# One feature-first token tile instead of two, in the value and output projections of a hybrid decoder layer

## The chip, the core and the metric

The kernel runs on one core of one Trainium2 chip. The time is the device time of one execution in microseconds. Five engines work side by side: TensorE (PE, with its weight loads PEld), VectorE (DVE), ScalarE (ACT), GpSimd (POOL) and SyncE (SP), which issues the transfers.

## The reference

One layer of a decoder is computed for 512 prompt tokens and 8 sample tokens, model width 1024. An input projection gives, per token, queries, keys, values and a gate for two mixers. Mixer A is gated linear attention (4 heads, keys of 64, values of 128, `va` with 512 columns), mixer B is dilated sliding-window attention (8 heads of 64, `vb` with 512 columns), for the samples against a cache of past keys and values. Each mixer's output is multiplied by the SiLU of its gate, the two are put side by side, and an output projection of 1024 x 1024, a residual and a LayerNorm follow:

```
h = x @ w_in;  qa, ka, va, za, ga, qb, kb, vb, gb = split(h)
o_a = rms_norm(gla(qa, ka, va, log_a(za))) ;  o_b = dilated_attention(qb, kb, vb)
y = concat(o_a * silu(ga), o_b * silu(gb)) @ w_out
x_new = layer_norm(ALPHA * x + y) ;  also out: new GLA states, kb, vb
```

## The kernel before

All operands lie in fast memory once loaded; x stands transposed, 1024 features in eight groups of 128 partitions, and 520 columns of tokens: prompt tiles 0 and 1 (256), the 8 samples, prompt tiles 2 and 3 (256). The first 264 columns are `TS[0]`, the last 256 `TS[1]`.

Precision comes from splitting: every weight and activation is a sum of a high and a low part, and each product is three matmuls (`three`, L622): high by high, high by low, low by high. So one unit of a projection is 8 x 3 = 24 matmuls that add up in one bank of the accumulator memory.

A unit has one of two forms. *Features first*: 128 weight columns are the stationary operand, the tokens move, and the result stands with features on the partitions. *Tokens first*: 128 tokens are stationary, 256 or 512 weight columns move, and the result stands with tokens on the partitions. Queries, keys and gates are features first throughout. The values are wanted tokens first for the prompt, but features first for the samples. `token` (L640) makes a group of 256 value columns (there are two of mixer B, `vb`, and two of mixer A, `va`): two units features first over `TS[0]`, whose prompt part of 256 columns `turn` (L659) copies out and turns by two transposes on TensorE, and two units tokens first for tiles 2 and 3. `va_into` and `vb_into` (L1085, L1102) copy the results to where the mixers read them; `vb_into` also splits them and stores them.

The output projection has the same two forms. `out_first` (L1512) runs eight units features first over tiles 0 and 1 and the samples (`ps_yf`), the first five of them in two halves: their products with mixer B's outputs ahead of all products with mixer A's. `out_turn` (L1533) copies, turns and adds them to the residual. `out_unit` (L1500) makes tiles 2 and 3 tokens first (`ps_y`, 512 or 256 columns); `out_evac` adds a result to the residual and takes its statistics; `norm` finishes a tile.

The generator `dense` (L695) gives the order of TensorE's large work: first keys and queries, then qb, kb, vb, gb, va, ga, then the output projection. All other work (decay, levels, scores, softmax, samples) stands in generators of its own with a priority from the table `PRIO` (L72). A planner (`Plan.run`, L308) builds the program: it keeps an estimated clock for each engine, charges each operation a cost (for a matmul in L120), and at each step records the operation that can start first, the smaller number in `PRIO` first among equals. `FROM_POOL` and `LATE` (L76, L78) are two of its waiting times. What it records is the fixed order on each engine; L368 is the line that records, and so nearly every row of the profile has that line. Accumulator banks have tags: three of "d" and three of "s" for products and scores, two of "t" for transposes and small results; the transposes of the probabilities (`ps_pt`) are of the latter.

Of the kernel before, what the change touches and what calls it, by code (L numbers as in the profile page):

```python
# [20 lines left out]
P = 128  # L21
# [48 lines left out]


PRIO = dict(  # L72
    wload=3, wsplit=4, decay=48.3, res_s=8, res=8, level=22, keys_out=2, logit=25.7, value=20, fills=9, bias_table=7.3, gla_levels=7.6, gla_diagonal=7.7, gla_state=24, gla_queries=25, strips=14, sample_queries=48, sample_softmax=8.7, sample_values=46, sample_gla=11, mix_sample_a=8.7, mix_sample_b=16, ln_rows=17, keys_store=17.5, gla_out=26, sample_v=9.2, mix_tiles=33.5, scores=31, softmax=34.2, weighted=30, mix_a=18, mix_b=19, norm3=11, norm=9)


FROM_POOL = 1000.0  # L76
TO_PE, FROM_PE, OTHER, AFTER_DMA, WITHIN = 600.0, 250.0, 150.0, 500.0, 120.0
LATE = 600.0  # L78
SWITCH = 230.0
PIECE = 256  # L80

# [114 lines left out]
class Plan:  # L196
# [14 lines left out]
    def add(self, gen, prio):  # L211
        self.seq += 1
        self.tasks.append(Task(gen, prio, self.seq))

    def mark(self, name):
        self.marks[name] += 1
# [156 lines left out]
def trunk(ctx: ExitStack, tc: tile.TileContext, xT, xp, xs, state, ck, cv, w_in, wab, gnorm,  # L373
# [17 lines left out]
    def bank(tag, name):  # L391
        return Need(tag, name, [P, 512])
# [20 lines left out]
    def copy(o, x):  # L413
        return V.tensor_copy(o, x), S.copy(o, x)
# [36 lines left out]
    def make(key, need, n=1):  # L451

        B[key] = yield need
        if n > 1:
            plan.share(B[key], n)
        mark(key)
# [165 lines left out]
    def three(ps, k, pairs):  # L622
        for i, (l, r) in enumerate(pairs):
            yield T.matmul(ps, l, r, start=k == 0 and i == 0, stop=k == KT - 1 and i == 2)
# [12 lines left out]
            add(evac(ps, u), 2)  # L637
        g.done(0)

    def token(g, evac_f, evac):  # L640

        for f in range(2):
            fs = slice(f * P, f * P + P)
            ps = yield bank("d", f"ps_{g.name}f{f}")
            for k in range(KT):
                yield g.at(k)
                h, l = xh[k][:, TS[0]], xl[k][:, TS[0]]
                yield from three(ps[:, :TW[0]], k, ((g.hi[k][:, fs], h), (g.hi[k][:, fs], l), (g.lo[k][:, fs], h)))
            add(evac_f(ps, f), 2)
        for t in (2, 3):  # L650
            ps = yield bank("d", f"ps_{g.name}{t}")
            ts = slice(NB + t * P, NB + t * P + P)
            for k in range(KT):
                yield from three(ps[:, :GW], k, ((xh[k][:, ts], g.hi[k]), (xh[k][:, ts], g.lo[k]), (xl[k][:, ts], g.hi[k])))
            add(evac(ps[:, :GW], t), 2)
        g.done(0)
        g.done(1)

    def turn(ps):  # L659

        f = yield Need("t1", "feat", [P, GW])
        yield copy(f, ps[:, :GW])
        free(ps)
        o = yield bank("t", "ps_turn")
        for t in range(2):
            yield T.transpose(o[:, t * P:t * P + P], f[:, t * P:t * P + P], ident)
        return o, f

    def sample_rows(x, rows):

# [24 lines left out]
    def dense():  # L695
# [44 lines left out]
        for t in range(TT):  # L740
            add(residual(t), PRIO["res"])
        add(residual_sample(), PRIO["res_s"])
        units = [(g, f) for g in range(4) for f in range(2)]
        yield from out_first(*units[:5])
        for x in units[5:]:
            yield from out_first(x)
        for t, c, w in ((2, 0, 512), (2, 512, 512), (3, 0, 512), (3, 512, GW), (3, 768, GW)):
            yield from out_unit(t, c, w)
# [316 lines left out]
    def keys_store():  # L1065

        yield At("kw", 8)
        yield At("y0_done", 1)
        for i in range(2):
            kw = B[f"kw{i}"].rearrange("p m (b j) -> p m b j", j=32)  # L1070
            for m in range(2):
                for a in range(4):
                    c = (2 * i + m) * P + a * 32
                    yield D.dma_start(kw_p[:, c:c + 32].rearrange("(b i) j -> i b j", i=32), kw[a * 32:a * 32 + 32, m])
            free(B[f"kw{i}"])
# [7 lines left out]
        mark(n + "_out")  # L1083

    def va_into(i):  # L1085
        def evac_f(ps, f):
            c = slice(i * GW + f * P, i * GW + f * P + P)
            yield copy(vat[:, 2 * i + f, :], ps[:, GW:TW[0]])
            mark("vat")
            ps, f_t = yield from turn(ps)  # L1090
            free(f_t)
            yield copy(B["va0"][:, :, c], ps[:, :GW].rearrange("p (t c) -> p t c", t=2))
            mark("va_done")
            free(ps)

        def evac(ps, t):
            yield copy(B["va1"][:, t - 2, i * GW:i * GW + GW], ps)
            free(ps)
            mark("va_done")
        return evac_f, evac  # L1100

    def vb_into(i):  # L1102
        def parts_of(o, x):
            yield S.copy(o[..., 0, :], x)
            yield V.tensor_tensor(o[..., 1, :], x, o[..., 0, :].bitcast(F32), op=ALU.subtract)

        def evac_f(ps, f):
            c = slice(i * GW + f * P, i * GW + f * P + P)
            yield copy(vnt[:, 2 * i + f, :], ps[:, GW:TW[0]])
            mark("vnt")  # L1110
            ps, raw = yield from turn(ps)
            yield from parts_of(B[f"vhl{i}0"][:, :, 2 * f:2 * f + 2], ps[:, :GW].rearrange("p (t h d) -> p t h d", t=2, d=64))
            mark(f"vb{i}0")
            yield copy(raw, ps[:, :GW])
            free(ps)
            yield D.dma_start(vw_p[:GW, c].rearrange("(t p) c -> p t c", p=P), raw.rearrange("p (t c) -> p t c", t=2))
            free(raw)

        def evac(ps, t):
            yield from parts_of(B[f"vhl{i}1"][:, t - 2], ps.rearrange("p (h d) -> p h d", d=64))  # L1120
            mark(f"vb{i}1")
            raw = yield Need("t1", "vb_raw", [P, GW])
            yield copy(raw, ps)
            free(ps)
            yield D.dma_start(vw_p[t * P:t * P + P, i * GW:i * GW + GW], raw)
            free(raw)
        return evac_f, evac


    def strips():  # L1130
# [347 lines left out]


    def ln_rows():  # L1480
        yield At("y0_done", 1)
        for n, src in (("gamma", ln_g), ("beta", ln_b)):
            B[n] = yield Need("g", n, [P, DM])
            yield D.dma_start(B[n], src.to_broadcast([P, DM]))
            mark("ln")
        yield S.mul(B["gamma"], B["gamma"], -0.5)
        mark("ln")
# [9 lines left out]
        yield D.dma_start(y, xp[t * P:t * P + P, :])  # L1497
        mark(f"y{t}")

    def out_unit(t, c, w):  # L1500
        u, tl, cs = t // 2, slice((t % 2) * P, (t % 2) * P + P), slice(c % 512, c % 512 + w)
        g = wo[c // 512]
        ps = yield bank("d", f"ps_y{t}{c // GW}")
        for k in range(KT):
            yield g.at(k)
            yield At(f"mix_b{u}{k}") if k < 4 else At(f"mix_a{u}", t % 2 + 1)
            mh, ml = (B[f"m{x}{'ba'[k // 4]}{u}"][:, k % 4, tl] for x in "hl")
            hi, lo = g.hi[k][:, cs], g.lo[k][:, cs]
            yield from three(ps[:, :w], k, ((mh, hi), (mh, lo), (ml, hi)))
        add(out_evac(t, c // GW, ps[:, :w]), 2)  # L1510

    def out_first(*units):  # L1512


        ps = []
        for g, f in units:
            ps.append((yield bank(("d", "s"), f"ps_yf{g}{f}")))
            yield from out_half(g, f, ps[-1], range(4))
        for (g, f), p in zip(units, ps):
            yield from out_half(g, f, p, range(4, KT))  # L1520
            add(out_turn(g, f, p), 2)

    def out_half(g, f, ps, ks):
        w, c = wo[g // 2], g % 2 * GW + f * P
        for k in ks:
            yield w.at(k)
            yield At(f"mix_b0{k}") if k < 4 else At("mix_a0", 2)
            yield At(f"mix_s{'ba'[k // 4]}")
            mh, ml = (B[f"m{x}{'ba'[k // 4]}0"][:, k % 4, :] for x in "hl")
            hi, lo = w.hi[k][:, c:c + P], w.lo[k][:, c:c + P]  # L1530
            yield from three(ps[:, :TW[0]], k, ((hi, mh), (lo, mh), (hi, ml)))

    def out_turn(g, f, ps):  # L1533
        feat = yield Need("t1", "feat_y", [P, GW])
        yield copy(feat, ps[:, :GW])
        yield copy(yts[:, 2 * g + f, :], ps[:, GW:TW[0]])
        mark("yts")
        free(ps)
        if f == 0:
            yield from make(f"yt{g}", bank("t", f"ps_yt{g}"))  # L1540
        else:
            yield At(f"yt{g}")
        for t in range(2):
            yield T.transpose(B[f"yt{g}"][:, t * GW + f * P:t * GW + f * P + P], feat[:, t * P:t * P + P], ident)
        free(feat)
        mark(f"yt_in{g}")
        if plan.marks[f"yt_in{g}"] == 2:
            plan.share(B[f"yt{g}"], 2)
            for t in range(2):
                add(out_evac(t, g, B[f"yt{g}"][:, t * GW:t * GW + GW]), 2)  # L1550

    def out_evac(t, g, ps):
        yield At(f"y{t}")
# [218 lines left out]
```

## Time and profile before

| | |
|---|---|
| time, median of 3 runs | 288.28 us (288.16 to 288.7) |
| the profiled execution, its own time | 287.84 us |
| its span, first to last instruction | 286.1 us |
| TensorE busy | 274.8 us, 96%, 2638 matmuls |
| VectorE busy | 223.5 us, 78% |
| ScalarE busy | 172.1 us, 60% |
| GpSimd busy | 59.6 us, 21% |
| mean granted TensorE clock | 0.997 of full speed |

A row of the profile that groups or lists instructions has the engine, the operation, what it writes `<-` what it reads, and the size: `128*128` is the stationary operand in rows and columns, `128x264` the partitions and columns that a matmul writes. A matmul's recorded duration contains the way through its pipeline, and several are under way at once; how fast they follow is the distance from start to start. The chain that ended last lists pieces of the critical chain as start, length, engine, tile and number of instructions.

### The profile page before, as it was taken

How to read it: one execution, taken by the hardware profiler on the slowest of the kernel's cores; microseconds unless marked ns; L12 is line 12 of the kernel's file. 1: busy time of each engine (PE TensorE's matmuls, PEld its weight loads, DVE VectorE, ACT ScalarE, POOL GpSimd, SP SyncE). 2: the span in 40 equal slices, each digit the busy share in tenths (PEclk: the TensorE clock that was granted, in tenths of full speed). 3: DMA queues.
4: the chain of work that ended last, by engine and by line, in shares of the span. 5: the costliest groups of instructions: out<-in, count | busy, mean ns of one | idle time of the engine just before them, and what ended most of it. 6: DMA issues, size and time to landing. Idle time of an engine off the chain costs nothing.

```text
span 286.1 us, 6902 instructions
## 1 busy us (share of the span) xinstructions
PE 274.8 (96%) x2638; PEld 259.1 (91%) x2638; DVE 223.5 (78%) x546; ACT 172.1 (60%) x481; POOL 59.6 (21%) x74
## 2 busy tenths in 40 slices
PE   8999999999999999999999999899999999999991
PEld 5999999999989899998999999799899999997890
DVE  4923887899999989989889897765698895439845
ACT  5726565456877887696888685435689774212002
POOL 4000000002945907200047635540000000000000
PEclk9999999999999999999999999999999999999998
DMA  6963643337738687527996858768193796751112
GB/s 205 341 167 93 203 111 105 91 110 221 244 88 297 194 256 240 159 83 214 264 235 200 261 157 231 198 169 229 52 255 115 208 313 236 124 170 73 78 76 92
DMA packets 58371, 51.20 MB, mean 179 GB/s; under 512 B 12750, under 2 KB 49752, under 8 KB 58338
## 3 DMA queue, kind: packets, MB, share of 16 engines
q1 hardware_dynamic: 57778, 50.36, 59.7%
q8 instruction: 21, 0.34, 0.5%
q10 hardware_dynamic: 560, 0.39, 0.4%
q14 instruction: 12, 0.10, 0.1%
HBM read 45.19 MB, written 6.05 MB: 179 GB/s over the span
## 4 chain that ended last, share of the span: by engine, by line
PE 67%; DVE 17%; ACT 9%; DMA 3%; issue 1%; SPq 1%; DVEq 0%; ACTq 0%
PE ps_qb L368 8%; PE ps_y L368 8%; PE ps_yf L368 7%; PE ps_gb L368 6%; PE ps_first L368 5%; PE ps_vb_f L368 4%; PE ps_vb L368 4%; PE ps_va L368 3%; PE ps_pv L368 3%; PE ps_pt L368 3%; PE ps_kb L368 2%; PE ps_qa L368 2%; ACT sg L368 2%; PE ps_s L368 2%; DMA raw_wo__3550<-in_w_out_dram 2%
## 5 line engine op out<-in xcount | busy, mean ns | idle before, releaser
L368 POOL TENSOR_TENSOR past<-past,qbc 128x256 f32<-128x256 f32 x32 | 29.0, 941 | 78.5 <-DMA past<-in_ck_dram 78.5
L368 POOL TENSOR_TENSOR vv<-vv,pb 128x256 f32<-128x256 f32 x32 | 26.3, 853 | 47.5 <-DVE gb_s L368 30.6
L368 ACT ACTIVATE pr<-pr,ms 128x128 f32<-128x128 f32 (+3 forms) x59 | 30.8, 548 | 4.5 <-DVE ms L368 4.4
L368 PE MATMUL ps_first<-xx,hi_first 128*128 128x264 f32 (+1 forms) x96 | 18.2, 289 | 0.4 <-DVE xx L368 0.3
L368 PEld LDWEIGHTS ps_first<-xx,hi_first 128*128 128x128 f32 x96 | 15.0, 190 | 1.4 <-DVE xx L368 0.5
L368 PE MATMUL ps_pt<-cf,pr 128*128 128x128 f32 x80 | 13.8, 280 | 1.2 <-DVE va L368 0.6
L368 DVE CUSTOM_DVE_ANT_0 pr<-ps_s,strip 128x128 f32<-128x128 f32 (+3 forms) x32 | 14.3, 479 | 0.0
L368 PE MATMUL ps_first<-xx,lo_first 128*128 128x264 f32 (+1 forms) x48 | 13.5, 282 | 0.0
L368 ACT ACTIVATE sg<-sg 128x264 f32<-128x264 f32 (+1 forms) x32 | 13.4, 418 | 0.2
L368 ACT ACTIVATE rstd<-mv,eps 128x1 f32<-128x1 f32 x4 | 1.1, 291 | 18.6 <-DVE mv L368 18.6
L368 PEld LDWEIGHTS ps_pt<-cf,pr 128*128 128x128 f32 x80 | 9.1, 140 | 2.4 <-ACT pr L368 1.2
L368 DVE TENSOR_TENSOR ptl<-ps_pt,pth 128x384 fp32r<-128x384 f32 (+1 forms) x16 | 9.7, 618 | 1.9 <-ACT pth L368 1.8
L368 ACT ACTIVATE d<-d 128x512 f32<-128x512 f32 x13 | 7.7, 636 | 5.1 <-DVE d L368 5.1
L368 DVE TENSOR_REDUCE o_pv<-vv 128x4 f32<-128x1024 f32 x8 | 9.7, 1212 | 0.6 <-POOL vv L368 0.6
L368 DVE TENSOR_REDUCE lt<-past 128x16 f32<-128x1024 f32 x8 | 9.6, 1210 | 0.0
L368 DVE TENSOR_TENSOR d<-b 128x1024 f32<-128x1024 f32 x7 | 9.0, 1290 | 0.0
L368 DVE TENSOR_TENSOR obT<-ps_pv,pvl 64x256 f32<-64x256 f32 x16 | 6.6, 415 | 3.0 <-ACT pvl L368 2.9
L368 PEld LDWEIGHTS ps_first<-xx,lo_first 128*128 128x128 f32 x48 | 9.0, 188 | 0.0
L368 ACT COPY feat_y<-ps_yf 128x256 f32<-128x256 f32 x7 | 2.6, 373 | 10.6 <-PE ps_yf L368 10.6
L368 PE MATMUL ps_s<-kp,qh 64*128 64x128 f32 (+3 forms) x64 | 8.5, 345 | 0.0
L368 ACT CAST pth<-ps_pt 128x384 fp32r<-128x384 f32 (+1 forms) x16 | 8.2, 532 | 0.1
L368 PE MATMUL ps_pv<-pth,vhl 128*128 128x256 f32 (+1 forms) x32 | 7.7, 272 | 0.0
(542 smaller groups left out, 1067.8 us busy)
## 6 DMA issues: line engine op xcount, KB each, us to landing
past<-in_ck_dram SPq DMA_DIRECT2D x8, 512.0 KB
vv<-in_cv_dram SPq DMA_DIRECT2D x8, 512.0 KB, 4.9
pb<-psd_s SPq DMA_DIRECT2D x16, 256.0 KB, 4.2
qbc<-qsd SPq DMA_DIRECT2D x8, 256.0 KB, 5.5
strip<-tabr SPq DMA_DIRECT2D x8, 256.0 KB, 3.1
y<-in_xp_dram SPq DMA_DIRECT2D x4, 512.0 KB
x_raw<-in_xT_dram SPq DMA_DIRECT2D x7, 260.0 KB
out_dram<-y SPq DMA_DIRECT2D x3, 512.0 KB, 2.6
```

What stands on the lines that cost most here:

```text
L368: getattr(eng.eng, op.fn)(*op.args, **op.kw)
```

## The change

The feature-first units of the values and of the output projection cover tile 1 and the samples, 136 columns, where they covered tiles 0 and 1 and the samples, 264. Tile 0 is made tokens first. `turn` now handles 128 prompt columns and one transpose; two feature units of a group share one accumulator bank for their transposes, and one evacuation of 256 columns follows. In the output projection the first five units are tile 0's first 512 columns and feature units 0 to 3, the other five tile 0's second 512 columns and feature units 4 to 7. Two waits on `y0_done` count to 3 in place of 1. All entries of `PRIO` but one and two of the planner's waiting times have other values, and the fixed order of every engine is recorded anew.

```diff
 PRIO = dict(
-    wload=3, wsplit=4, decay=48.3, res_s=8, res=8, level=22, keys_out=2, logit=25.7, value=20, fills=9, bias_table=7.3, gla_levels=7.6, gla_diagonal=7.7, ...
+    wload=12.1, wsplit=5.9, decay=31.1, res_s=18.3, res=28.2, level=22.5, keys_out=2, logit=35.7, value=28.9, fills=59.4, bias_table=37.7, gla_levels=11.8, gla_diagonal=17.1, ...
-FROM_POOL = 1000.0
+FROM_POOL = 300.0
-LATE = 600.0
+LATE = 900.0
...
-    def token(g, evac_f, evac):
+    def token(g, own, evac):
         for f in range(2):
             fs = slice(f * P, f * P + P)
             ps = yield bank("d", f"ps_{g.name}f{f}")
             for k in range(KT):
                 yield g.at(k)
-                h, l = xh[k][:, TS[0]], xl[k][:, TS[0]]
-                yield from three(ps[:, :TW[0]], k, ((g.hi[k][:, fs], h), (g.hi[k][:, fs], l), (g.lo[k][:, fs], h)))
-            add(evac_f(ps, f), 2)
-        for t in (2, 3):
+                h, l = xh[k][:, P:TW[0]], xl[k][:, P:TW[0]]
+                yield from three(ps[:, :P + NB], k, ((g.hi[k][:, fs], h), (g.hi[k][:, fs], l), (g.lo[k][:, fs], h)))
+            add(turn(g.name, ps, f, own[:, f, :], evac), 2)
+        for t in (0, 2, 3):
...
-    def turn(ps):
-        f = yield Need("t1", "feat", [P, GW])
-        yield copy(f, ps[:, :GW])
+    def turn(n, ps, f, own, evac):
+        feat = yield Need("t1", "feat", [P, P])
+        yield copy(feat, ps[:, :P])
+        yield copy(own, ps[:, P:P + NB])
+        mark("vnt" if n[1] == "b" else "vat")
         free(ps)
-        o = yield bank("t", "ps_turn")
-        for t in range(2):
-            yield T.transpose(o[:, t * P:t * P + P], f[:, t * P:t * P + P], ident)
-        return o, f
+        if f == 0:
+            yield from make("turn_" + n, bank("t", "ps_turn"))
+        else:
+            yield At("turn_" + n)
+        o = B["turn_" + n]
+        yield T.transpose(o[:, f * P:f * P + P], feat, ident)
+        free(feat)
+        if f:
+            add(evac(o[:, :GW], 1), 2)
...
-        units = [(g, f) for g in range(4) for f in range(2)]
-        yield from out_first(*units[:5])
-        for x in units[5:]:
+        yield from out_first((0, 0), 0, 1, 2, 3)
+        for x in ((0, 512), 4, 5, 6, 7):
             yield from out_first(x)
...
     def out_first(*units):
         ps = []
-        for g, f in units:
-            ps.append((yield bank(("d", "s"), f"ps_yf{g}{f}")))
-            yield from out_half(g, f, ps[-1], range(4))
-        for (g, f), p in zip(units, ps):
-            yield from out_half(g, f, p, range(4, KT))
-            add(out_turn(g, f, p), 2)
+        for ks in range(4), range(4, KT):
+            for i, x in enumerate(units):
+                if ks[0] == 0:
+                    ps.append((yield bank(("d", "s"), f"ps_yf{i}")))
+                if isinstance(x, tuple):
+                    yield from out_unit(*x, 512, ps[i], ks)
+                else:
+                    yield from out_half(x, ps[i], ks)
...
-            yield from three(ps[:, :TW[0]], k, ((hi, mh), (lo, mh), (hi, ml)))
+            yield from three(ps[:, :P + NB], k, ((hi, mh), (lo, mh), (hi, ml)))
```

The recorded order shows the new sequence. On TensorE, around the turns of the first group of mixer B's values (`ps_vb_f` is the second feature unit, `ps_vb_2` and `ps_vb_0` are token units of tiles 2 and 0, `xx` are the parts of x, `hi_vb` and `lo_vb` those of the weights), before:

```order
L368 MATMUL ps_vb_f_1630<-xx_179,hi_vb__1212 128x264
L368 MATMUL ps_turn<-cf,feat 128x128 x2
L368 MATMUL ps_vb_f_1630<-xx_178,lo_vb__1213 128x264
...
L368 MATMUL ps_vb_f_1630<-xx_263,lo_vb__1433 128x264
L368 MATMUL ps_vb_2_1684<-hi_vb__1212,xx_107 128x256
...
L368 MATMUL ps_turn<-cf,feat 128x128 x2
L368 MATMUL ps_vb_2_1684<-hi_vb__1432,xx_219 128x256
```

And with the change:

```order
L368 MATMUL ps_vb_f_1622<-xx_219,lo_vb__1449 128x136
L368 MATMUL ps_turn<-cf,feat 128x128
L368 MATMUL ps_vb_f_1622<-xx_219,hi_vb__1448 128x136
...
L368 MATMUL ps_vb_f_1622<-xx_263,lo_vb__1449 128x136
L368 MATMUL ps_vb_0_1660<-hi_vb__1318,xx_107 128x256
...
L368 MATMUL ps_turn<-cf,feat 128x128
L368 MATMUL ps_vb_0_1660<-hi_vb__1318,xx_178 128x256
```

Nine matmuls of the second feature unit and nine of tile 0's unit now stand between the two transposes; before, two transposes stood at each place, with the rest of the unit and half of tile 2's between. Over the four groups TensorE has 192 matmuls of 136 columns in place of 192 of 264, 96 more of 256, and 8 transposes fewer.

On TensorE, where the output projection begins (`mhb`, `mlb` are the parts of mixer B's gated outputs, `ps_oat` turns mixer A's), before:

```order
L368 MATMUL ps_yf_3652<-mhb_2263,hi_wo__3318 128x264
L368 MATMUL ps_yf_3652<-mhb_2263,lo_wo__3319 128x264
L368 MATMUL ps_yf_3652<-mlb_2264,hi_wo__3318 128x264
...
L368 MATMUL ps_oat<-cf,oa_3144 128x128 x8
L368 MATMUL ps_yf_3686<-mlb_2264,hi_wo__3336 128x264
...
L368 MATMUL ps_yf_3652<-mha_3608,hi_wo__3502 128x264
```

And with the change:

```order
L368 MATMUL ps_yf_3732<-hi_wo__3441,mhb_2261 128x512
L368 MATMUL ps_yf_3732<-lo_wo__3442,mhb_2261 128x512
L368 MATMUL ps_yf_3732<-hi_wo__3441,mlb_2262 128x512
...
L368 MATMUL ps_oat<-cf,oa_3238 128x128 x8
...
L368 MATMUL ps_yf_3790<-mhb_2261,hi_wo__3441 128x136
...
L368 MATMUL ps_yf_3732<-hi_wo__3628,mha_3700 128x512
```

The first unit is tile 0's first half, tokens first (the outputs are now the stationary operand), and four of 136 columns follow before mixer A's products. Over the projection there are 192 matmuls of 136 columns in place of 192 of 264, 48 more of 512, and 8 transposes fewer.

More of the change, by code (lines that the diff above doesn't have):

```diff
@@ L72 @@
 PRIO = dict(
-    wload=3, wsplit=4, decay=48.3, res_s=8, res=8, level=22, keys_out=2, logit=25.7, value=20, fills=9, bias_table=7.3, gla_levels=7.6, gla_diagonal=7.7, gla_state=24, gla_queries=25, strips=14, sample_queries=48, sample_softmax=8.7, sample_values=46, sample_gla=11, mix_sample_a=8.7, mix_sample_b=16, ln_rows=17, keys_store=17.5, gla_out=26, sample_v=9.2, mix_tiles=33.5, scores=31, softmax=34.2, weighted=30, mix_a=18, mix_b=19, norm3=11, norm=9)
-FROM_POOL = 1000.0
+    wload=12.1, wsplit=5.9, decay=31.1, res_s=18.3, res=28.2, level=22.5, keys_out=2, logit=35.7, value=28.9, fills=59.4, bias_table=37.7, gla_levels=11.8, gla_diagonal=17.1, gla_state=27, gla_queries=21.6, strips=26.7, sample_queries=8.4, sample_softmax=8.4, sample_values=38.6, sample_gla=7.7, mix_sample_a=4.9, mix_sample_b=14.8, ln_rows=8.4, keys_store=17.1, gla_out=17.7, sample_v=26.4, mix_tiles=27.7, scores=39.6, softmax=27.8, weighted=50.7, mix_a=38.6, mix_b=57.6, norm3=8.7, norm=15.3)
+FROM_POOL = 300.0
 TO_PE, FROM_PE, OTHER, AFTER_DMA, WITHIN = 600.0, 250.0, 150.0, 500.0, 120.0
-LATE = 600.0
+LATE = 900.0
 SWITCH = 230.0
@@ L646, in token @@
                 yield g.at(k)
-                h, l = xh[k][:, TS[0]], xl[k][:, TS[0]]
-                yield from three(ps[:, :TW[0]], k, ((g.hi[k][:, fs], h), (g.hi[k][:, fs], l), (g.lo[k][:, fs], h)))
-            add(evac_f(ps, f), 2)
-        for t in (2, 3):
+                h, l = xh[k][:, P:TW[0]], xl[k][:, P:TW[0]]
+                yield from three(ps[:, :P + NB], k, ((g.hi[k][:, fs], h), (g.hi[k][:, fs], l), (g.lo[k][:, fs], h)))
+            add(turn(g.name, ps, f, own[:, f, :], evac), 2)
+        for t in (0, 2, 3):
             ps = yield bank("d", f"ps_{g.name}{t}")
-            ts = slice(NB + t * P, NB + t * P + P)
+            o = NB * (t > 1) + t * P
+            ts = slice(o, o + P)
             for k in range(KT):
@@ L1067, in keys_store @@
         yield At("kw", 8)
-        yield At("y0_done", 1)
+        yield At("y0_done", 3)
         for i in range(2):
@@ L1085, in va_into, with evac @@
     def va_into(i):
[L1086 to L1094, printed above, removed]
         def evac(ps, t):
-            yield copy(B["va1"][:, t - 2, i * GW:i * GW + GW], ps)
+            yield copy(B[f"va{t // 2}"][:, t % 2, i * GW:i * GW + GW], ps)
             free(ps)
             mark("va_done")
-        return evac_f, evac
+        return vat[:, 2 * i:2 * i + 2, :], evac
     def vb_into(i):
-        def parts_of(o, x):
+        def evac(ps, t):
+            o, x = B[f"vhl{i}{t // 2}"][:, t % 2], ps.rearrange("p (h d) -> p h d", d=64)
             yield S.copy(o[..., 0, :], x)
             yield V.tensor_tensor(o[..., 1, :], x, o[..., 0, :].bitcast(F32), op=ALU.subtract)
[L1107 to L1121, printed above, removed]
+            mark(f"vb{i}{t // 2}")
             raw = yield Need("t1", "vb_raw", [P, GW])
@@ L1126, in evac @@
             free(raw)
-        return evac_f, evac
+        return vnt[:, 2 * i:2 * i + 2, :], evac
     def strips():
@@ L1480, in ln_rows @@
     def ln_rows():
-        yield At("y0_done", 1)
+        yield At("y0_done", 3)
         for n, src in (("gamma", ln_g), ("beta", ln_b)):
@@ L1498, in residual, with out_unit @@
         mark(f"y{t}")
-    def out_unit(t, c, w):
+    def out_unit(t, c, w, ps=None, ks=range(KT)):
         u, tl, cs = t // 2, slice((t % 2) * P, (t % 2) * P + P), slice(c % 512, c % 512 + w)
         g = wo[c // 512]
-        ps = yield bank("d", f"ps_y{t}{c // GW}")
-        for k in range(KT):
+        ps = ps or (yield bank("d", f"ps_y{t}{c // GW}"))
+        for k in ks:
             yield g.at(k)
@@ L1509, in out_unit, with out_half @@
             yield from three(ps[:, :w], k, ((mh, hi), (mh, lo), (ml, hi)))
-        add(out_evac(t, c // GW, ps[:, :w]), 2)
+        if KT - 1 in ks:
+            add(out_evac(t, c // GW, ps[:, :w]), 2)
     def out_first(*units):
         ps = []
-        for g, f in units:
-            ps.append((yield bank(("d", "s"), f"ps_yf{g}{f}")))
-            yield from out_half(g, f, ps[-1], range(4))
-        for (g, f), p in zip(units, ps):
-            yield from out_half(g, f, p, range(4, KT))
-            add(out_turn(g, f, p), 2)
-    def out_half(g, f, ps, ks):
-        w, c = wo[g // 2], g % 2 * GW + f * P
+        for ks in range(4), range(4, KT):
[6 more added lines that the diff above has]
+                    yield from out_half(x, ps[i], ks)
+    def out_half(m, ps, ks):
+        w, c = wo[m // 4], m % 4 * P
         for k in ks:
@@ L1528, in out_half, with out_turn @@
             yield At(f"mix_s{'ba'[k // 4]}")
-            mh, ml = (B[f"m{x}{'ba'[k // 4]}0"][:, k % 4, :] for x in "hl")
+            mh, ml = (B[f"m{x}{'ba'[k // 4]}0"][:, k % 4, P:] for x in "hl")
             hi, lo = w.hi[k][:, c:c + P], w.lo[k][:, c:c + P]
-            yield from three(ps[:, :TW[0]], k, ((hi, mh), (lo, mh), (hi, ml)))
[L1533 to L1536, printed above, removed]
+            yield from three(ps[:, :P + NB], k, ((hi, mh), (lo, mh), (hi, ml)))
+        if KT - 1 in ks:
+            add(out_turn(m, ps), 2)
+    def out_turn(m, ps):
+        feat = yield Need("t1", "feat_y", [P, P])
+        yield copy(feat, ps[:, :P])
+        yield copy(yts[:, m, :], ps[:, P:P + NB])
         mark("yts")
         free(ps)
-        if f == 0:
-            yield from make(f"yt{g}", bank("t", f"ps_yt{g}"))
-        else:
-            yield At(f"yt{g}")
-        for t in range(2):
-            yield T.transpose(B[f"yt{g}"][:, t * GW + f * P:t * GW + f * P + P], feat[:, t * P:t * P + P], ident)
+        n = f"yt{m // 2}"
+        if m % 2 == 0:
+            yield from make(n, bank("t", "ps_" + n))
+        else:
+            yield At(n)
+        yield T.transpose(B[n][:, m % 2 * P:m % 2 * P + P], feat, ident)
         free(feat)
[L1546 to L1550, printed above, removed]
+        mark(n + "_in")
+        if plan.marks[n + "_in"] == 2:
+            add(out_evac(1, m // 2, B[n][:, :GW]), 2)
     def out_evac(t, g, ps):
```

## The prediction

> **What bounds the kernel now.** I read the page's busy shares first, then TensorE's waits, then the busy time by stage, then the chain that ended last.
>
> ```profile
> PE 274.8 (96%) x2638; PEld 259.1 (91%) x2638; DVE 223.5 (78%) x546; ACT 172.1 (60%) x481; POOL 59.6 (21%) x74
> PEclk9999999999999999999999999999999999999998
> ```
>
> TensorE (PE) works almost from end to end at its full granted clock, and there are as many weight loads (PEld) as matmuls: each of the 2638 matmuls brings its own stationary operand in, even where two in a row use the same one. The next view is who TensorE waited for.
>
> ```profile
> PE ps_va_f L368 <- DVE lo_va__2973 L368: 1.2, 2, 1.0
> PE warm_ps L368 <- DVE warm L1640: 1.2, 1, 1.2
> PE ps_pt L368 <- DVE va L368: 0.6, 1, 0.6
> PE ps_oa L368 <- DVE oa L368: 0.6, 1, 0.6
> PE ps_pt L368 <- DVE pt L368: 0.5, 1, 0.5
> PE ps_first L368 <- DVE xx L368: 0.3, 1, 0.3
> PE ps_yf L368 <- DVE ga L368: 0.3, 1, 0.3
> ```
>
> That is every wait over 150 ns: 1.2 + 1.2 + 0.6 + 0.6 + 0.5 + 0.3 + 0.3 = 4.7 us in all, 1.8 of it around the GLA values (the first and third rows). So TensorE is the bound in every stage; VectorE is the next one. The stages (values of mixer B 93.5 to 126.5, values of mixer A 162.5 to 195.5, output projection 232.7 to 278.8, then the tail):
>
> ```profile
> core 0: us, PE busy (x) PEld busy (x) DVE busy (x) ACT busy (x) POOL busy (x), PEclk, DMA share, GB/s
> 93.50:126.50 33.00, 32.97 (x281) 31.78 (x282) 29.34 (x84) 26.99 (x84) 13.85 (x16) 1.00 0.64 197
> 126.50:162.50 36.00, 36.00 (x299) 33.84 (x299) 32.13 (x83) 29.07 (x74) 11.43 (x14) 1.00 0.76 214
> 162.50:195.50 33.00, 31.13 (x257) 30.19 (x255) 25.15 (x44) 18.07 (x46) 14.91 (x19) 1.00 0.72 203
> 195.50:232.70 37.20, 36.43 (x343) 34.93 (x341) 30.55 (x107) 29.41 (x106) 0.00 (x0) 1.00 0.64 175
> 232.70:278.80 46.10, 46.03 (x311) 42.04 (x312) 29.11 (x76) 10.71 (x32) 0.00 (x0) 1.00 0.46 145
> 278.80:286.10 7.30, 0.99 (x10) 0.42 (x9) 4.13 (x9) 1.64 (x6) 0.00 (x0) 0.89 0.26 90
> ```
>
> In the stages that the change touches TensorE is idle for 0.03, 1.87 and 0.07 us. Whatever the change adds to TensorE's stream there lengthens the run, up to those waits.
>
> **The price of one matmul.** A matmul's recorded duration contains its pipeline, so I price by distance from start to start, taken from unbroken pieces of the chain that ended last (start, length, matmuls).
>
> ```profile
> 99.78 1.58 PE ps_vb_f L368 x13
> 101.35 1.42 PE ps_vb L368 x12
> 142.35 0.44 PE ps_pt L368 x4
> 240.61 1.46 PE ps_yf L368 x12
> 242.28 1.45 PE ps_yf L368 x12
> 261.81 16.97 PE ps_y L368 x96
> ```
>
> Features first with 264 moving columns: 1.58/13 = 0.1215 us for values, 1.46/12 = 0.1217 for the output. Tokens first with 256 columns: 1.42/12 = 0.118. A transpose (128 columns): 0.44/4 = 0.11; the 0.21 us between the two ps_yf pieces, 240.61 + 1.46 to 242.28, are two more of them. The ps_y piece is 48 matmuls of 512 columns and 48 of 256: (16.97 - 48 x 0.118)/48 = 0.2356 for 512.
>
> No matmul of 136 columns with a 128-wide stationary operand stands in this stream, and the whole answer hangs on its price. By columns alone it would be far below 0.12. But each brings a weight load, and the trace has one place where loads come closer together than usual: in a weighted-values unit, two short matmuls (128 columns) are followed by a long one. First the loads, then the matmuls, in order of time.
>
> ```profile
> 144.96 0.19 PEld L368 LDWEIGHTS ps_pv<-pth,vhl 128*128 128x128 f32 x1
> 145.08 0.13 PEld L368 LDWEIGHTS ps_pv<-ptl,vhl 128*64 128x64 f32 x1
> 145.14 0.19 PEld L368 LDWEIGHTS ps_pv<-pth,vhl 128*128 128x128 f32 x1
> 145.25 0.19 PEld L368 LDWEIGHTS ps_pv<-ptl,vhl 128*128 128x128 f32 x1
> 145.37 0.19 PEld L368 LDWEIGHTS ps_pv<-pth,vhl 128*128 128x128 f32 x1
> ...
> 145.08 0.22 PE L368 MATMUL ps_pv<-pth,vhl 128*128 128x128 f32 x1
> 145.14 0.22 PE L368 MATMUL ps_pv<-ptl,vhl 128*64 128x128 f32 x1
> 145.20 0.33 PE L368 MATMUL ps_pv<-pth,vhl 128*128 128x256 f32 x1
> 145.37 0.28 PE L368 MATMUL ps_pv<-ptl,vhl 128*128 128x256 f32 x1
> ```
>
> The two short matmuls start 0.06 us apart, which is what the columns alone cost. The load between them is only 64 wide (0.13 against 0.19 us: 64 columns fewer take 0.06 less). The next load is 128 wide; it starts at 145.14, the one behind it not before 145.25, and the matmul that needs it lasts 0.33 instead of 0.28: it stood 0.05 us waiting for its operand. So 128-wide loads follow each other at 0.11 us, one after the other, and a matmul whose columns take less than that is paced by them. The scores give a second witness: pairs of half-height tiles, 128 wide, 128 moving columns, where the two of a pair start together.
>
> ```profile
> 95.02 0.27 PE L368 MATMUL ps_s<-kp,ql 64*128 64x128 f32 x2
> 95.12 0.34 PE L368 MATMUL ps_s<-kp,qh 64*128 64x256 f32 x2
> ```
>
> The pair of 128 columns at 95.02 is followed by the next one 0.10 to 0.11 us later, not 0.06. The transposes, 128 columns on a 128-wide operand, come at 0.11 too. I take **0.11 us for 136 columns**; the ends are 0.06 (columns alone) and 0.12 (as 264 columns now). The row nearest in kind, the same data type and a 128-wide load, is the 0.11.
>
> **The sum.** The order of the changed kernel has 192 matmuls 128x136 for the values in place of 192 128x264, 96 more of 128x256, and 8 transposes fewer; for the output 192 of 128x136 in place of 192 of 128x264, 48 more of 128x512, and 8 transposes fewer. Nothing else on TensorE changes in number; so the change does what it says.
>
> Values: 192 x (0.11 - 0.1215) = -2.2; 96 x 0.118 = +11.3; 8 x 0.11 = -0.9; together +8.2 us, half of it in each value stage. Output: 192 x (0.11 - 0.1217) = -2.2; 48 x 0.2356 = +11.3; -0.9; together +8.2 us. The columns streamed are the same, 192 x 264 = 50,688 for the values before and 192 x 136 + 96 x 256 = 50,688 after; but the feature-first matmul gets hardly cheaper when it is halved, and the tile that left it must be paid again. Total **+16.4 us**, as 384 p - 25.8 with p the price of a 136-column matmul.
>
> Off TensorE: the copies that feed the transposes are half as wide, one evacuation of 512 columns takes the place of two of 256, and the value stores are 256 columns wide instead of twice 128. All lies beside a busy TensorE (VectorE 29.34 of 33.00 us and 29.11 of 46.10 us in two of the stages), so I price it at nothing; if that cover were gone it would be a gain of at most the copies' own time. The longer TensorE stream gives VectorE and ScalarE time: I let 2.2 of the 4.7 us of waits go, the 1.8 of the GLA values and some of the rest. What is late next is nothing new: in the output stage TensorE alone is busy to the end, and the tail after it is untouched.
>
> The new table of priorities moves much of the order. I put its effect at nothing, with bounds from the waits: at best all 4.7 us go, at worst as much again comes. Its planner charges a 136-column matmul 136 x 0.4167 + 11 = 68 ns (L120); by the rows above TensorE will run later than planned, so the other engines will rather be ahead of it than behind. The DMA issues keep nearly their sequence: the weight groups stand among the same transfers, a few places earlier or later.
>
> Profiled execution 287.84 + 16.4 - 2.2 = 302.0; the median of the runs lies 0.44 over the profiled one, so **302.5 us**. With the bounds: 304.7 - 4.7 = 300.0 to 304.7 + 4.7 = 309.4.
>
> **Rivals.** *Columns set the pace (faster).* If the loads were hidden behind the matmuls, as the first short pair at 0.06 suggests, p = 0.06 gives 384 x 0.06 - 25.8 = -2.8, thus 285.5 us. It decides as soon as p is below 25.8/384 = 0.067 us. Against it: the pair hides a load of half the width, and the debt is paid by the next matmul. 5%.
>
> *A middle pace.* A stream of load and matmul could run half way between the two, at 0.085 us: the sum is 384 x 0.085 - 25.8 = +6.8 and the time 287.84 + 0.44 + 6.8 - 2.2 = 292.9 us. For it: loads may be pulled further ahead over a long stream than these short stretches show. Against it: in the transposes and the scores they are not. 5%.
>
> The Trainium skill's page "TensorE: Matmul & The Clock Gate" gives a pace of that kind in its section "Back-to-back issue gap": about 81 ns for 128 columns in a sustained stream of load and matmul; its section on LDWEIGHTS has columns/1.2, 107 ns for 128, and the trace's 0.11 stands with the latter; no run so far shows the former.
>
> *The value stages hide their share.* If VectorE's chain from the values to the attention outputs were the true bound between 93 and 195 us, only the output's +8.2 would show: 287.84 + 0.44 + 8.2 = 296.5 us. For it: the chain that ended last runs through DVE and ACT for stretches there, and DVE is busy 32.13 of 36.00 us. Against it: TensorE is busy 36.00 of the same 36.00. 6%.
>
> *The bank of the transposes.* The change holds one of the two "t" banks from the first feature unit's transpose to behind the second's: 9 matmuls at 0.11, 9 at 0.118 and a transpose in the order shown, 2.2 us, in each of four groups, and the probabilities' transposes need those banks. Were each hold to become idle time of TensorE with some 0.4 us of evacuation, it would cost 4 x 2.6 = 10.4 us: 312.9 us. Against it: TensorE has value matmuls to run meanwhile. 6%.
>
> **How the numbers follow.** The forecast has 75%, its own range 300 to 309. Other accidents of the new order: 3%. About 0.2% (0.6 us) is what a measurement of this kernel can tell from no change. Faster: the first rival and a sliver, 6%; within it 1%; slower 93%. The range reaches down to the third rival, 296, and ends at the forecast's upper bound, 309.
>
> **What would show it.** In the changed profile, loads of ps_vb_f, ps_va_f and the 136-column ps_yf at 0.11 us from start to start, 24 of them in 2.6 us; stages of the values some 4 us longer each and the output stage some 8; no new wait over 1 us on TensorE. A pace of 0.06 to 0.07 there makes the prediction wrong in its sign; a pace of 0.11 with the stages not longer makes TensorE the wrong bound.

## The result and the profile after

| | before | changed |
|---|---|---|
| median | 288.22 us (4 runs) | 299.65 us (299.18 to 300.03, 4 runs) |
| ratio | | 1.0395, 95% interval 1.0368 to 1.0421 |
| profiled execution, span | 287.84, 286.1 us | 300.03, 298.2 us |

The change makes the kernel slower by 11.4 us (12.1 us between the spans of the two profiled executions). The forecast was 302.5 us in a range of 296 to 309. The busy shares of the changed kernel's page:

```profile
PE 289.6 (97%) x2766; PEld 273.8 (92%) x2766; DVE 224.9 (75%) x555; ACT 167.9 (56%) x470; POOL 54.9 (18%) x74
PEclk9999999999999999999999999999999999999998
```

TensorE has the 128 more matmuls that the order showed (144 added, 16 transposes fewer), 14.8 us more busy time, and still its full clock. Who it waited for:

```profile
PE warm_ps L368 <- DVE warm L1626: 1.2, 1, 1.2
PE ps_l L368 <- DVE near L368: 0.5, 1, 0.5
PE ps_first L368 <- DVE xx L368: 0.3, 1, 0.3
PE ps_pt L368 <- DVE ptl L368: 0.2, 1, 0.2
```

2.2 us in place of 4.7; both waits around mixer A's values are gone. The stages (values of mixer B, gates of mixer B, values of mixer A, gates of mixer A, output projection, tail; columns as in the prediction's table by stage):

```profile
95.20:130.70 35.50, 35.42 (x311) 34.67 (x310) 27.57 (x70) 23.19 (x69) 14.67 (x20) 1.00 0.75 222
130.70:170.50 39.80, 39.62 (x333) 37.54 (x332) 37.94 (x100) 33.41 (x85) 11.45 (x16) 1.00 0.71 199
170.50:200.80 30.30, 30.30 (x267) 30.29 (x266) 17.26 (x32) 11.04 (x28) 11.61 (x15) 1.00 0.78 212
200.80:233.30 32.50, 32.50 (x314) 31.37 (x313) 28.39 (x96) 26.42 (x97) 3.78 (x3) 1.00 0.60 156
233.30:291.00 57.70, 57.70 (x385) 51.59 (x383) 35.10 (x86) 13.79 (x42) 0.00 (x0) 1.00 0.48 142
291.00:298.20 7.20, 0.96 (x10) 0.42 (x8) 4.11 (x9) 1.64 (x6) 0.00 (x0) 0.88 0.26 91
```

The stages' borders have moved, since softmax work that stood among the values is now done in the stage of mixer B's gates (of the probabilities' transposes 14 lay among mixer A's values and 4 do now); so a stage is no measure of its own units, and the sign that the prediction named, value stages some 4 us longer each, can't be read here. What stays is that TensorE is busy all through: 30.30 of 30.30 and 57.70 of 57.70 us, and in mixer A's values the weight loads fill the stage as well, 30.29 of 30.30. The tail is 7.20 us, where it was 7.30. The pieces of the chain that price the units:

```profile
171.82 2.64 PE ps_va_f L368 x24
193.35 7.54 PE ps_va L368 x64
261.02 2.64 PE ps_yf L368 x24
```

A unit of 24 matmuls of 136 columns takes 2.64 us, 0.11 each, for values and output alike; 256 columns take 7.54/64 = 0.118. In the list of instructions by time, loads and matmuls of such a unit:

```profile
172.00 0.30 PEld L368 LDWEIGHTS ps_va_f<-xx,hi_va__2720 128*128 128x128 f32 x2
172.22 0.19 PEld L368 LDWEIGHTS ps_va_f<-xx,lo_va__2721 128*128 128x128 f32 x1
172.33 0.30 PEld L368 LDWEIGHTS ps_va_f<-xx,hi_va__2720 128*128 128x128 f32 x2
172.56 0.19 PEld L368 LDWEIGHTS ps_va_f<-xx,lo_va__2721 128*128 128x128 f32 x1
...
172.06 0.39 PE L368 MATMUL ps_va_f<-xx,hi_va__2720 128*128 128x136 f32 x2
172.28 0.28 PE L368 MATMUL ps_va_f<-xx,lo_va__2721 128*128 128x136 f32 x1
172.39 0.39 PE L368 MATMUL ps_va_f<-xx,hi_va__2720 128*128 128x136 f32 x2
172.62 0.27 PE L368 MATMUL ps_va_f<-xx,lo_va__2721 128*128 128x136 f32 x1
```

Three loads from 172.00 to 172.33 and three from 172.22 to 172.56: one each 0.11 us, and the matmuls in the same step.

To see where the 12.1 us of span went, I summed for every matmul the distance from its start to the next one's, by the tile that it writes. This counts a stall with the matmul that it follows, and a late load with the matmul ahead of the one that needs it. In us:

| tiles | before | changed | difference |
|---|---|---|---|
| values: feature units, token units, their transposes (`ps_vb_f`, `ps_va_f`, `ps_vb`, `ps_va`, `ps_turn`) | 27.50 + 23.67 + 1.33 | 21.73 + 35.03 + 0.37 | +4.6 |
| output over tiles 0 and 1 and the samples, its transposes (`ps_yf`, `ps_yt`) | 24.77 + 1.17 | 33.02 + 0.40 | +7.5 |
| all others | 199.9 | 199.9 | 0.1 |

The sum is +12.2, the whole loss, and it is the sum of the units that the change touches: mixer B's values +4.0, mixer A's +1.6, their transposes -1.0, the output +7.5. The other tiles only balance out: `ps_l` grew from 7.24 to 8.01 us, `ps_first` from 18.69 to 19.36, while `ps_oa` fell from 6.32 to 5.49 and `ps_pt` from 7.71 to 7.22.

### The profile page after: what moved, and what is told of

It is laid out like the page before. It is cut to its first block, busy times and chain, and to the rows that moved or that the text cites. A ratio compares the mean times of both kernels' runs of the same rounds, so it can differ in the third digit from the quotient of the medians.

```text
span 298.2 us, 7162 instructions
## 1 busy us (share of the span) xinstructions
PE 289.6 (97%) x2766; PEld 273.8 (92%) x2766; DVE 224.9 (75%) x555; ACT 167.9 (56%) x470; POOL 54.9 (18%) x74
## 4 chain that ended last, share of the span: by engine, by line
PE 77%; DVE 11%; DMA 5%; ACT 3%; issue 1%; POOL 1%; SPq 1%; DVEq 0%; POOLq 0%; ACTq 0%
PE ps_yf L368 11%; PE ps_ga L368 8%; PE ps_qb L368 8%; PE ps_y L368 8%; PE ps_vb L368 6%; PE ps_va L368 6%; PE ps_first L368 5%; PE ps_va_f L368 4%; PE ps_vb_f L368 3%; PE ps_kb L368 3%; PE ps_gb L368 3%; DVE pr L368 2%; PE ps_qa L368 2%; PE ps_oa L368 2%; PE ps_pt L368 2%; PE ps_pv L368 2%
## 5 line engine op out<-in xcount | busy, mean ns | idle before, releaser
L368 ACT ACTIVATE pr<-pr,ms 128x256 f32<-128x256 f32 (+3 forms) x52 | 27.5, 549 | 5.3 <-DVE ms L368 5.0
L368 POOL TENSOR_TENSOR past<-past,qbc 128x256 f32<-128x256 f32 x32 | 23.8, 781 | 33.7 <-DMA past<-in_ck_dram 33.7
L368 PE MATMUL ps_first<-xx,hi_first 128*128 128x264 f32 (+1 forms) x96 | 18.9, 298 | 0.3 <-DVE xx L368 0.3
L368 PEld LDWEIGHTS ps_first<-xx,hi_first 128*128 128x128 f32 x96 | 15.7, 197 | 1.2 <-DVE xx L368 0.6
L368 ACT COPY feat_y<-ps_yf 128x128 f32<-128x128 f32 x7 | 1.9, 266 | 19.9 <-PE ps_yf L368 19.9
L368 POOL MEMSET att<- 64x512 f32 x2 | 1.0, 522 | 57.3 <-DVE ks L368 57.3
L368 ACT COPY pvl<-ps_pv 64x256 f32<-64x256 f32 x16 | 5.6, 370 | 5.6 <-PE ps_pv L368 5.3
```

Of the source, the lines that this page charges most:

```text
L368: getattr(eng.eng, op.fn)(*op.args, **op.kw)
```

## The experiments

Theory at the start: a 136-column matmul costs a weight load, 0.11 us, and TensorE's stream sets the time. The changed kernel came out 2.9 us faster than that theory's forecast, so the first four runs separate the units from the new table of priorities.

**The new table with the old units.**

```diff
 (before)
-PRIO = dict(wload=3, wsplit=4, decay=48.3, ...)
-FROM_POOL = 1000.0
-LATE = 600.0
+PRIO = dict(wload=12.1, wsplit=5.9, decay=31.1, ...)
+FROM_POOL = 300.0
+LATE = 900.0
```

> The kernel before (features first over two tiles and the samples, 264 columns) with the changed kernel's table of priorities and its two waiting times alone; all is computed. Theory A, the units cost 16.4 us on TensorE and the new table gives back what the change fell short of that: 288.2 + 11.4 - 16.4 = 283 us, 282 to 286. Theory B, the table does nothing by itself and the longer TensorE stream is what swallowed the waits: 287.5 to 289.5. Theory C, the table is part of the loss: over 290.

Measured 291.96 us, ratio to before 1.0102 (1.0064 to 1.0141). With the old units the new table costs 3.6 us, by the interval 1.8 to 4.1. Theory A, that the table is a gain by itself, is out by 9 us. The number is theory C's. TensorE's waits in this run (its whole list has 6.7 us):

```profile
PE ps_ort L368 <- DVE o_r L368: 1.0, 1, 1.0
PE ps_turn L368 <- ACT feat L368: 1.0, 1, 1.0
PE ps_pt L368 <- DVE obT L368: 1.0, 1, 1.0
PE ps_gb L368 <- DVE ms L368: 0.6, 2, 0.3
```

TensorE stands here in front of work for which the changed kernel lists no wait, the copy ahead of the value transposes among it.

**The old table with the new units.**

```diff
 (changed kernel)
-PRIO = dict(wload=12.1, ...);  FROM_POOL = 300.0;  LATE = 900.0
+PRIO = dict(wload=3, ...);  FROM_POOL = 1000.0;  LATE = 600.0
```

> The changed kernel's units (136 columns) with the table of priorities and the waiting times of the kernel before; all is computed. Theory A: 288.2 + 16.4 less the waits that a longer TensorE stream swallows, 302 to 305 us. Theory B, the waits go by themselves: 299 to 301, like the changed kernel. Theory C, the new table is part of the loss: under 299.

Measured 303.3 us, 1.0512 (1.0488 to 1.0536): the units alone cost 15 us, and the new table takes 3.65 us off that. The number is theory A's: theory C falls here, as theory A fell above. Each table is good for its own units and bad for the others', by about the same 3.6 us. In the sums by tile, this run's value units stand at 57.21 us and its output units at 33.40, within 0.1 of the changed kernel's; the 2.6 us between the two spans (300.8 and 298.2) lie in other tiles: transposes of probabilities 8.28 against 7.22, keys 25.58 against 24.94, gates of mixer B 25.12 against 24.65, scores 9.55 against 9.14; `ps_l` goes the other way, 7.25 against 8.01. The list of waits hardly shows them:

```profile
PE warm_ps L368 <- DVE warm L1626: 1.2, 1, 1.2
PE ps_pt L368 <- DVE pt L368: 0.5, 1, 0.5
PE ps_vb_f L368 <- DVE kw L368: 0.3, 1, 0.3
PE ps_vb_f L368 <- DVE lo_vb__1848 L368: 0.2, 1, 0.2
```

2.2 us, as in the changed kernel. So the difference lies in stalls that this view does not list, or lists at less than they cost (an example stands in the part on why the prediction was right).

**The values alone, and the output alone, with the old table.**

```diff
 (before)   values alone
-                h, l = xh[k][:, TS[0]], xl[k][:, TS[0]]
+                h, l = xh[k][:, P:TW[0]], xl[k][:, P:TW[0]]
 ... token, turn, va_into and vb_into as changed; out_first as before
 (before)   output alone
-        yield from out_first(*units[:5])
+        yield from out_first((0, 0), 0, 1, 2, 3)
 ... out_unit, out_first, out_half, out_turn as changed; token as before
```

> The kernel before with the change in the value projections alone, old table; all is computed. If TensorE is the bound there, +8.2 us of matmuls less at most the 1.8 us of waits at mixer A's values: 294.5 to 297 us. The rival that VectorE's chain hides the added matmuls expects 288 to 290.

> The kernel before with the change in the output projection alone, old table; all is computed. TensorE is alone in that stage: +8.2 us, 295.5 to 297.5 us. The rival that 136 columns are priced by their columns (0.06 us) expects 192 x (0.06 - 0.1217) + 11.3 - 0.9 = -1.4 us, 287 us.

Measured 296.94 us (ratio 1.0313, 1.0254 to 1.0373) and 296.0 us (1.0257, 1.0237 to 1.0278). Against the 288.35 us of before in these runs that is +8.6 and +7.65 us, for 8.2 expected of each, and together, 16.2, somewhat more than the 15 us of both in one kernel. The rival that VectorE's chain hides the values (288 to 290 us) and the one that columns set the price (287 us) are both out. By tiles, the output's units cost +7.7 us in the second run, all of it. In the first the values' units cost only +4.7 us, as in the changed kernel; another 1.3 us stands at the output's matmuls, 1.0 at the gates of mixer B and 0.7 at the probabilities' transposes. So that 8.6 lies near 8.2 is in part chance.

**200 columns in place of 136, order unchanged.** The disputed cost by itself: 64 columns more per feature-first matmul, in both projections.

```diff
 (changed kernel)
-                h, l = xh[k][:, P:TW[0]], xl[k][:, P:TW[0]]
-                yield from three(ps[:, :P + NB], ...)
+                h, l = xh[k][:, P - 64:TW[0]], xl[k][:, P - 64:TW[0]]
+                yield from three_as(ps[:, :64 + P + NB], ..., P + NB)   # charged as 136
-        yield copy(feat, ps[:, :P])
+        yield copy(feat, ps[:, 64:64 + P])
```

> The changed kernel, but its 384 feature-first matmuls move 200 columns, not 136: 64 columns of tile 0 come along and their results are not used. The planner charges as for 136, so the order of every engine stays as it was. If the weight load sets the pace at 0.11 us, the added columns fit under it (200 columns at the 264-column rate of 0.1215/264 are 0.092 us): 299 to 300.5 us. If the pace goes with the columns, 64 more cost 64 x 0.1215/264 = 0.029 us each, 384 x 0.029 = 11.3 us: 311 us.

Measured 299.65 us, the changed kernel's median; to the hundredth by chance, since the kernel before ran at 287.66 us beside this run and at 288.22 beside that one. The chain's piece for a unit:

```profile
171.44 2.66 PE ps_va_f L368 x24
```

0.111 us each: 24,576 more columns moved (384 x 64) for next to nothing. By tiles the 384 matmuls took 43.8 us, 43.2 in the changed kernel.

**264 columns, order unchanged.**

```diff
 (changed kernel, as the run above)
-    P - 64 ... 64 + P
+    P - 128 ... 128 + P
```

> The changed kernel, but its feature-first matmuls move 264 columns as before the change, of which only the 136 of tile 1 and the samples are used; order of every engine unchanged. If the load's 0.11 us is a floor under the columns, 264 columns cost their 0.1215 us again: 384 x (0.1215 - 0.112) = +3.6 us over the changed kernel, 303 to 304 us. If the price goes with the columns from 136 on: 384 x 128 x 0.1215/264 = +22.6 us, 322 us.

Measured 303.94 us, 4.3 over the changed kernel, where 3.6 was expected:

```profile
172.64 2.92 PE ps_va_f L368 x24
```

0.1217 us each, the price of before. So the price is flat from 136 to 200 columns and is set by the columns at 264: a floor of 0.11 us under them.

**Two halves with 64 weight columns each.** What is the floor: the load, or something that each matmul costs?

```diff
 (changed kernel)
+            ops = [T.matmul(ps[:64, j * W2:j * W2 + W2], l[:, j * 64:j * 64 + 64], r, start=..., stop=...) for j in range(2)]
+            for op in ops:
+                op.cost /= 2
+            yield Batch(ops)
```

> The changed kernel, but each feature-first matmul is made as two, with 64 weight columns as the stationary operand each; the halves' results lie side by side in the bank and the copies out are two of 64 partitions. All is computed. If 128-wide loads set the pace, a 64-wide load takes half (0.055 us) and the columns of a half 0.06: a pair takes 0.12 us, 384 x 0.01 = +4 us, 302 to 306 us. If each matmul has a fixed floor of 0.11 us whatever it loads, a pair takes 0.22: +42 us, 342 us.

Unlike the expectation says, not all is computed as meant: the sums of the feature-first units, the only ones touched, come out wrong. Both halves start their sum in the same bank; that the second start loses part of the first half is a guess that no run tests. The number and kind of the matmuls are as meant. Measured 311.27 us (ratio 1.0819, 1.0783 to 1.0855), between the two expectations and far from the 342 of a floor for each matmul. A piece of the chain:

```profile
189.74 5.14 PE ps_va_f L368 x80
```

And TensorE's longest wait:

```profile
PE ps_yf L368 <- ACT hi_wo__4285 L368: 1.7, 1, 1.7
```

One half takes 5.14/80 = 0.064 us. A matmul of 136 columns costs 0.064 with a 64-wide load and 0.112 with a 128-wide one; the floor is the load. A pair costs 0.128 in place of the expected 0.12, which makes 384 x (0.128 - 0.112) = 6.1 of the 11.6 us over the changed kernel. The planner recorded another order here, and about half of the rest lies where TensorE waits for the output weights: by tiles the output's 48 matmuls of 512 columns took 14.2 us in place of 11.5.

**The planner told of the floor.**

```diff
 (changed kernel)
-                c = ... else max(n, 64) * .4167 + 11
+                c = ... else max(max(n, 64) * .4167 + 11, m * .83 + 5)
```

> The changed kernel, its planner charging a matmul at least the time of its weight load (128 x 0.83 + 5 = 111 ns in place of 68 ns for 136 columns); the order is recorded anew, all is computed. If TensorE has hardly a wait left to remove, nothing is won: 299 to 302 us. If the wrong price in the planner is part of the loss: under 298.

Measured 302.14 us, just over the first expectation, 2.5 slower than with the wrong price. With this table, the true price in the planner does not win the loss back. Whether another table would go better with it was not tried.

**The planner's waiting times, and the new table for the values alone.**

```diff
 (changed kernel)                        (values alone, as above)
-FROM_POOL = 300.0                       -PRIO = dict(wload=3, ...)
-LATE = 900.0                            +PRIO = dict(wload=12.1, ...)
+FROM_POOL = 1000.0                      +FROM_POOL = 300.0
+LATE = 600.0                            +LATE = 900.0
```

> The changed kernel with the planner's two waiting times (for GpSimd and for late transfers) as before the change, its new table of priorities kept; all is computed. If the table and the waiting times were fitted to these units together, part of the 3.65 us between the two tables is lost: 301 to 303 us. If the waiting times do not matter: 299 to 300.5 us.

> The kernel before with the change in the value projections alone, and the new table with its waiting times; all is computed. With the old table it took 296.94 us. If the new table's gain of 3.65 us belongs to the value stages: 293 to 294.5 us. If it fits only both changed projections together: 297 us or more.

Measured 300.58 us (299.77 to 300.61) and 294.32 us (1.0232, 1.0182 to 1.0282). The first lies between its two expectations; its lowest run is not above the changed kernel's highest, so the waiting times decide little. The second is 2.6 us below the same units with the old table, of the 3.65 us that the table is worth in all: most of the gain seems to go with the new value units, without the output's. The size is rough, as the four times of each of the two runs lie up to 2.6 and 3.5 us apart; but the tiles that gain are those of above (transposes of probabilities 8.41 to 7.23, keys 25.44 to 24.90, gates of mixer B 25.40 to 24.79, scores 9.78 to 9.13).

## Why the prediction was right

**The bound.** TensorE was the bound, and stayed it: 96% busy before, 97% after, with 2.2 us of listed waits.

**The price of 136 columns.** Taken as 0.11 us; it measured 0.11 in the chain, 0.112 as the middle of all distances. This was read from one place where a load of 128 columns followed a load of 64 and a matmul stood 0.05 us, from the transposes and from pairs of scores, and it was the whole sign: at 0.06 us the kernel would, by the prediction's sum, have been faster. (In a matmul's row the last pair, such as `128x136`, is the operand that moves; that it is also what is written holds only where the stationary operand is 128*128, not for the 128*64 there.) Runs with 200, 264 and twice 64 columns show that it is the load. The rival of a middle pace, 0.085 us, is out with the same rows. The Trainium skill's page "TensorE: Matmul & The Clock Gate", in its section "Back-to-back issue gap", gives about 81 ns for 128 columns in a stream of load and matmul; the trace has 0.11 us for 136 columns and for the transposes' 128, and the measurement decides.

**The added matmuls.** 96 x 0.118 = 11.3 us were expected for the values, and the token units grew by 35.03 - 23.67 = 11.4; for the output 11.3 for 48 matmuls of 512 columns, and they took 11.5 by tiles.

**The feature units of the values** are the term that was mis-sized. -2.2 us were put down for them, and 1.8 more of waits; they fell by 27.50 - 21.73 = 5.8 us. The 96 of mixer A alone took 14.64 us before, 0.1525 each in place of the 0.1215 of an undisturbed piece, and 10.70 after. Most of that excess is the waits that the prediction knew, at more than the list says. In the kernel before, by time:

```profile
184.01 0.40 PE L368 MATMUL ps_va_f<-xx,hi_va__2972 128*128 128x264 f32 x2
185.43 0.39 PE L368 MATMUL ps_va_f<-xx,lo_va__2973 128*128 128x264 f32 x1 [1.02 <-DVE lo_va__2973 L368]
185.66 0.29 PE L368 MATMUL ps_va_f<-xx,hi_va__2972 128*128 128x264 f32 x1
```

The second matmul of the pair starts at 184.13, the next at 185.43 and the one behind that at 185.66: 1.30 and 0.23 us where 0.12 is the step, 1.29 us lost. The list has 1.02, because it counts idle time from the end of a matmul's recorded duration, here 0.28 us behind its start. The three waits among these units (1.87 us of idle time) cost 2.6 us by such distances. The step of the prediction that failed is therefore the size of the waits that go: 2.2 us were let go at the list's price. Mixer B's feature units fell by another 1.8 us where 1.1 was expected; part of that is stalls too short for the list, such as 0.31 us from start to start at 93.94. The sums by tile are not exact about such short ones: of two transposes at 99.39 the second takes only 0.03 us and the matmul behind it 0.20, together with the first (0.11) the 0.34 of two transposes and one matmul, so part of the transposes' price is counted with the unit behind them.

**The output** cost 7.5 us by tiles and 7.7 us alone, for 8.2 expected.

**The new table** was put at nothing within 4.7 us either way. It gave 3.65 us to the new units. With the old table the time is 303.3 us, 0.8 over the forecast of 302.5; but that it is so near is partly luck. By tiles the touched units cost 12.1 or 12.2 us with either table, where 16.4 less the 1.8 of waits, 14.6, were expected; with the old table the other tiles took 2.5 us more than before (202.4 against 199.9), which the prediction did not have, and the two errors nearly cancel. With the new table the other tiles stand where they stood, and the units' error is what shows. Of the 2.85 us between forecast and median 0.8 more is the step from the profiled execution to the median: taken as +0.44 us, it was -0.38. The bounds held, but not for the reason given, the listed waits: these are 2.2 us with both tables. Why the table fits its own units is open: the difference is spread over many short stalls in the keys, scores and transposes, and no run singled one out.

**The bank of the transposes.** The changed kernel's one listed wait of a probabilities' transpose is 0.2 us, where the rival needs 10.4, and these transposes take less time by tiles than before (7.22 against 7.71 us). The rival is out.

**The planner's price.** I had expected its error to do no harm, and correcting it did not help with this table; that it was harmless because other engines run ahead was argued, not shown.

## What to carry to other kernels

Where each matmul brings its own stationary operand, as here, look for a floor under its price: the trace shows it as the distance between loads (0.11 us for loads 128 wide). In this kernel 136 columns cost what 200 do. Before splitting a wide unit into a narrow one and another form, price the narrow one by the load, and look for the rare place in the trace where loads come close enough to show their own pace. A list of waits is not all of an engine's lost time, since it has a lower limit and counts idle time from the end of the recorded matmul (1.02 us listed, 1.29 lost): divide a group's whole time by its number, and compare with an undisturbed piece.

## What the runs showed that I had not expected

A table of priorities that was worth 3.65 us with one form of units cost 3.6 us with the other, with the same amount of listed waiting (2.2 us) in two runs that differ by 2.6 us of span. And 64 more columns in each of 384 matmuls, which at the pace of columns would have cost 11.3 us, left the median at 299.65 us.
